# Half of the first weight loaded later, two warming products fewer, and norm factors by token turned from the finished row

## The chip, the core and the metric

The kernel runs on one core of one Trainium2 chip. The core has five engines, each with its own list of instructions that it works through in order: TensorE (PE, with PEld for the loading of its stationary operand), VectorE (DVE), ScalarE (ACT), GpSimd (POOL) and SyncE (SP, which here only issues transfers). They wait for each other on semaphores. The metric is the time of one execution on the device in microseconds (us). The kernel before took 2257.14 us, the median of three runs (2255.66 to 2258.51).

## What is computed

A decoder trunk of two layers over 1024 tokens of width 1024, with a memory of 256 tokens, all in float32. In short:

```
for l in (0, 1):
    if l == 1: shared K/V of the sparse attention = rmsnorm(x, g_kv) @ w_kv
    mem_k, mem_v = split(rmsnorm(mem, g_mem[l]) @ w_mem_kv[l])
    h = rmsnorm(x, g_mix[l])
    if l == 0:   # gated linear attention and memory attention
        q, k, v, r, alr, mq = split(h @ a_w_in)
        x = x + concat(gla(q, k, v, alr) * silu(r), mem_attend(mq)) @ a_w_out
    else:        # native sparse attention and memory attention
        x = x + concat(nsa(h, shared), mem_attend(mq)) @ b_w_out
    x = x + conv_ffn(rmsnorm(x, g_ffn[l]))
return rmsnorm(x, g_final)
rmsnorm(x, g) = x * rsqrt(mean(x * x, axis=-1) + 1e-6) * g
```

## The kernel before, in words

**Layout.** Activations lie with 128 channels on the partitions and tokens along the row: `x` is eight tiles (k = 0 to 7) of 128 channels by 1024 tokens, worked on in two halves of 512 tokens. Every operand of a dense product is split into a rounded high part and the rest (`rl`, `rl_into`, `wsplit`: ScalarE casts the high part, VectorE subtracts it), and each product is three matmuls: high by high, high by low, low by high. `projg` (L189) does this for one 128-column weight over the eight k: 24 matmuls of 128 by 512, lines L194 to L196.

**Norms.** The factor of a norm is not multiplied into the input of a product but into its output. `Norm` sums the squares of the eight tiles into two accumulators `nacc`. `done()` adds these, and one matmul with a matrix of 1/1024 (`on_d`, L287) leaves the mean square in the bank `ms`, 128 equal rows of 512 tokens. `inv_rms` (L243) makes the factors `rs` of it in six operations that each need the one before: Ln, Exp and Square on ScalarE (L246 to L248), then three on VectorE (L249 to L251).

Products whose output has tokens on the partitions (values) need the same factors as a column: `by_token` (L290) multiplies each 128 tokens of the accumulator with one column of `on_d`, four matmuls of one output column into a bank `mst`, and runs a second `inv_rms` on 128 by 4 (`rst`). It needs only the accumulator, not `rs`. The memory norm (`MemKV.norm`, L363) does it with two more columns in its own bank `mms`. There are six such places, lettered here by time in the profile:

- A, 27 us: `stats(0)`, first half of layer 0, L661 and L662, behind the third of four 24-matmul products `qk`, ahead of the fourth.
- B, 49 us: `stats(1)`, second half, between the value products `gv` of the first half.
- C, 72 us: memory norm of layer 0, between the products `mk`.
- D, 1046 us: `norm(0)` in `after_ffn0`, L1488, between the last products `dn` of the first feed-forward.
- E, 1067 us: `norm(1)`, behind the products `kc` of the first half, ahead of those of the second.
- F, 1093 us: memory norm of layer 1, behind the products `mk`, ahead of `mv`.

**The start.** PE first runs fourteen products of `on_d` with itself (`warm`, L146). `stats(0)` issues the loads on SP: x tile 0, the first half of the first weight `wqk`, x tile 1, the second half of that weight, x tiles 2 to 7. Then ScalarE and VectorE split both weight halves, and after them each x tile into `h` (L650 to L652). The first weight half holds k = 0 to 3, the second k = 4 to 7. The gain `cg` comes by ScalarE's queue.

**What sets the order.** A scheduler takes the program in the order in which it is written, with generators (`yield`) woven into each other by `blend`, and lays the instructions of each engine in a list; it may move one ahead of another whose inputs are not ready. PSUM banks come from one pool of eight (`PS`, L81), all with the tag `ps`, in the order in which the program takes them. At run time each engine follows its list.

## Time and profile before

| | |
|---|---|
| median of three runs | 2257.14 us (2255.66 to 2258.51) |
| profiled execution, first to last instruction | 2257.4 us |
| PE busy | 2215.0 us, 98% of the span |
| DVE, ACT, POOL busy | 1729.8, 1126.3, 433.6 us |
| mean granted clock of PE | 0.997 of full |
| PE's recorded waits for another engine or a transfer | about 30 us in all, the longest 2.67 us |

In a row of the timeline the first number is the start in us from the span's start, the second the busy time of the group; then engine, line, operation, output <- inputs, shape, count, and in brackets the idle time of that engine just before it with what ended it. Matmuls overlap: one of 128 by 512 shows 0.39 us, and the next starts 0.227 us after it; the distance of starts is what it costs. A float32 matmul that was not split stands as two.

### The profile page before, as it was taken

How to read it: one execution, taken by the hardware profiler on the slowest of the kernel's cores; microseconds unless marked ns; L12 is line 12 of the kernel's file. 1: busy time of each engine (PE TensorE's matmuls, PEld its weight loads, DVE VectorE, ACT ScalarE, POOL GpSimd, SP SyncE). 2: the span in 40 equal slices, each digit the busy share in tenths (PEclk: the TensorE clock that was granted, in tenths of full speed). 3: DMA queues.
4: the chain of work that ended last, by engine and by line, in shares of the span. 5: the costliest groups of instructions: out<-in, count | busy, mean ns of one | idle time of the engine just before them, and what ended most of it. 6: DMA issues, size and time to landing. Idle time of an engine off the chain costs nothing.

```text
span 2257.4 us, 31218 instructions
## 1 busy us (share of the span) xinstructions
PE 2215.0 (98%) x10994; PEld 1826.2 (81%) x10994; DVE 1729.8 (77%) x3069; ACT 1126.3 (50%) x2085; POOL 433.6 (19%) x409
## 2 busy tenths in 40 slices
PE   9999999999999999999999999999999999999997
PEld 7888887777888888888888878778777788888886
DVE  6786886888877768887756778866988877768877
ACT  5464464543333335456544788864543333334445
POOL 1222300013333210000103334420013333210000
PEclk9999999999999999999999999999999999999999
DMA  6332246333332329544421111036433333329533
GB/s 227 103 104 87 73 161 208 138 126 133 129 122 98 108 84 345 173 135 136 131 83 50 40 46 37 8 115 206 140 130 131 126 122 103 108 76 339 167 96 112
DMA packets 139451, 285.15 MB, mean 126 GB/s; under 512 B 16221, under 2 KB 22958, under 8 KB 139294
## 3 DMA queue, kind: packets, MB, share of 16 engines
q1 hardware_dynamic: 130942, 263.11, 35.5%
q0 software_dynamic: 3600, 11.65, 1.5%
q10 hardware_dynamic: 4752, 8.39, 1.0%
q8 instruction: 86, 1.41, 0.3%
q14 instruction: 71, 0.58, 0.1%
HBM read 211.27 MB, written 71.83 MB: 125 GB/s over the span
## 4 chain that ended last, share of the span: by engine, by line
PE 78%; DVE 10%; ACT 4%; DMA 4%; issue 2%; SPq 0%; POOL 0%; DVEq 0%; ACTq 0%; POOLq 0%
PE dn L1413 5%; PE dn L1414 5%; PE dn L1412 5%; PE fy L1058 5%; PE fy L1060 5%; PE fy L1059 5%; PE fx L1058 3%; PE fx L1059 3%; PE fx L1060 3%; PE fw L1060 3%; PE fw L1059 3%; PE fw L1058 3%; PE op L195 2%; PE op L196 2%; PE op L194 2%
## 5 line engine op out<-in xcount | busy, mean ns | idle before, releaser
L1413 PE MATMUL dn<-db,da 128*128 128x512 f32 (+1 forms) x628 | 242.5, 386 | 0.6 <-DVE db L1342 0.5
L1412 PE MATMUL dn<-db,da 128*128 128x512 f32 (+1 forms) x628 | 242.6, 386 | 0.2 <-ACT db L1341 0.2
L1414 PE MATMUL dn<-db,da 128*128 128x512 f32 (+1 forms) x628 | 241.7, 385 | 0.0
L1058 PE MATMUL fy<-B,Ah 128*128 128x512 f32 x496 | 194.6, 392 | 10.8 <-DVE q L1092 9.9
L1060 PE MATMUL fy<-B,Al 128*128 128x512 f32 x496 | 193.3, 390 | 0.4 <-DVE Al L1023 0.4
L1059 PE MATMUL fy<-B,Ah 128*128 128x512 f32 x496 | 193.1, 389 | 0.0
L1042 POOL TENSOR_TENSOR wu<-wu,wu 128x512 f32<-128x512 f32 x36 | 47.2, 1311 | 735.1 <-DVE Al L1023 600.5
L1022 ACT ACTIVATE Ah<-wu 128x1024 fp32r<-128x1024 f32 x124 | 130.4, 1052 | 102.8 <-PE fy L1059 60.3
L1023 DVE TENSOR_TENSOR Al<-wu,Ah 128x1024 fp32r<-128x1024 f32 x124 | 160.8, 1297 | 8.4 <-ACT Ah L1022 7.3
L1413 PEld LDWEIGHTS dn<-db,da 128*128 128x128 f32 x628 | 117.9, 188 | 26.8 <-DVE db L1342 2.8
L1412 PEld LDWEIGHTS dn<-db,da 128*128 128x128 f32 x628 | 118.0, 188 | 24.4 <-ACT db L1341 0.6
L1060 PE MATMUL fw<-B,Al 128*128 128x512 f32 x352 | 137.7, 391 | 0.0
L1058 PE MATMUL fw<-B,Ah 128*128 128x512 f32 x352 | 137.1, 390 | 0.0
L1059 PE MATMUL fw<-B,Ah 128*128 128x512 f32 x352 | 137.1, 389 | 0.0
L1414 PEld LDWEIGHTS dn<-db,da 128*128 128x128 f32 x628 | 117.9, 188 | 23.2
L1342 DVE TENSOR_TENSOR db<-bl,db 128x512 fp32r<-128x512 f32 x154 | 106.0, 688 | 28.4 <-ACT db L1341 27.9
L1058 PEld LDWEIGHTS fy<-B,Ah 128*128 128x128 f32 x496 | 93.1, 188 | 35.2 <-DVE q L1092 14.1
L1341 ACT ACTIVATE db<-bl 128x512 fp32r<-128x512 f32 x154 | 95.7, 621 | 31.3 <-PE dn L1414 20.6
L1060 PEld LDWEIGHTS fy<-B,Al 128*128 128x128 f32 x496 | 93.1, 188 | 20.6 <-DVE Al L1023 0.9
L1059 PEld LDWEIGHTS fy<-B,Ah 128*128 128x128 f32 x496 | 93.1, 188 | 18.9
L1138 ACT ACTIVATE fc<-fc 128x512 f32<-128x512 f32 x88 | 54.9, 626 | 106.3 <-DVE fc L1119 85.2
L1341 ACT ACTIVATE da<-wb 128x512 fp32r<-128x512 f32 x88 | 54.9, 628 | 101.4 <-PE dn L1413 63.9
(416 smaller groups left out, 6185.8 us busy)
## 6 DMA issues: line engine op xcount, KB each, us to landing
wu<-in_w_up_dram SPq DMA_DIRECT2D x176, 256.0 KB, 3.0
bl<-gb_d SPq DMA_DIRECT2D x154, 256.0 KB, 2.9
gb_d<-fc SPq DMA_DIRECT2D x132, 256.0 KB, 2.4
wb<-in_w_down_dram SPq DMA_DIRECT2D x44, 256.0 KB, 4.2
wa<-in_w_down_dram SPq DMA_DIRECT2D x22, 512.0 KB, 7.8
wo<-in_a_wo_dram SPq DMA_DIRECT2D x16, 512.0 KB, 3.7
xre<-om_d SPq DMA_DIRECT2D x32, 256.0 KB, 4.3
x_r<-x SPq DMA_DIRECT2D x32, 256.0 KB, 2.4
```

What stands on the lines that cost most here:

```text
L1022: a = nc.scalar.activation(hi, src, AF.Copy)
L1023: b = nc.vector.tensor_tensor(lo, src, f(hi), ALU.subtract)
L1042: tt(b1, b0, b1, ALU.add)
L1058: mm(ps, wr, hr, start=(first and j == 0), stop=False, skip_group_check=True)
L1059: mm(ps, wr, hl, start=False, stop=False, skip_group_check=True)
L1060: mm(ps, wl, hr, start=False, stop=(stop and j == 3), skip_group_check=True)
L1138: silu[0] = nc.scalar.activation(self.c[half], self.c[half], AF.Silu)
L1341: nc.scalar.activation(w[:, hs(0)], t, AF.Copy)
L1342: b = tt(w[:, hs(1)], t, f(w)[:, hs(0)], ALU.subtract)
L1412: mm(o, hi, bh, start=first, stop=False, skip_group_check=True)
L1413: mm(o, hi, bl, start=False, stop=False, skip_group_check=True)
L1414: mm(o, lo, bh, start=False, stop=stop or n == NP - 1, skip_group_check=True)
```

## The change

Three things. The load of the first weight's second half moves behind x tile 3, and its split stands just before the split of that tile, tied behind tile 2's on ScalarE. The warming products are twelve and no longer fourteen. And `by_token` becomes a function that takes the finished `rs`: TensorE turns each 128 by 128 piece of it (`transpose` with the identity, one matmul each), and VectorE copies one column of each piece out of the bank. The one-column matmuls and the second `inv_rms` are gone in all six places; the memory norm takes a bank `mst` of its own for it.

```diff
@@ -144,7 +144,7 @@
         )
 
     warm = PS("warm")
-    for _ in range(14):
+    for _ in range(12):
         mm(warm[:, :P], on_d, on_d, start=True, stop=True)
 
     def back_to_exp(after):
@@ -251,6 +251,14 @@
         nc.vector.tensor_tensor(y[:, :n], y[:, :n], a[:, :n], ALU.mult)
         return y
 
+    def by_token(rs, n):
+        pt = PS("mst")
+        for c in range(n):
+            nc.tensor.transpose(pt[:, c * P : (c + 1) * P], rs[:, c * P : (c + 1) * P], ident)
+        y = S([P, 4], s="rst", bufs=3)
+        nc.vector.tensor_copy(y[:, :n], pt[:, : n * P].rearrange("p (c q) -> p c q", c=n)[:, :, 0])
+        return y
+
     class Norm:
         def __init__(self, width=HT):
             self.acc = [None, None]
@@ -287,19 +295,6 @@
                 mm(ms, on_d, self.acc[j], start=(j == 0), stop=(j == n - 1))
             return inv_rms(ms, self.w)
 
-        def by_token(self):
-            n = self.w // P
-            pt = PS("mst")
-            for c in range(n):
-                for j, a in enumerate(self.acc):
-                    mm(
-                        pt[:, c : c + 1],
-                        a[:, c * P : (c + 1) * P],
-                        on_d[:, 0:1],
-                        start=(j == 0),
-                        stop=(j == len(self.acc) - 1),
-                    )
-            return inv_rms(pt[:, :n], n, S([P, 4], s="rst", bufs=3), S([P, 4], s="rtt", bufs=2))
 
     def gained(get, rs, gc, h, odd=(1, 3, 5, 7)):
         for k in range(KT):
@@ -365,9 +360,8 @@
             acc = self.acc
             ms = PS("mms")
             mm(ms[:, :M], on_d, acc[:, :M], start=True, stop=True)
-            for m in range(2):
-                mm(ms[:, M + m : M + m + 1], acc[:, m * P : (m + 1) * P], on_d[:, 0:1], start=True, stop=True)
-            self.rs = inv_rms(ms[:, : M + 2], M + 2)
+            self.rs = inv_rms(ms[:, :M], M)
+            self.rst = by_token(self.rs, 2)
 
         def project(self):
             M = 256
@@ -406,7 +400,7 @@
                         mm(pv[m], hl, r, start=False, stop=(k == KT - 1))
                     yield 1.3
             for m in range(2):
-                self.V.append(rl(pv[m], scale=self.rs[:, M + m : M + m + 1], s="mV"))
+                self.V.append(rl(pv[m], scale=self.rst[:, m : m + 1], s="mV"))
 
     om_d = dp.tile([KT, P, T], F32, name="om_d")
     x_r = dp.tile([KT, P, T], F32, name="x_r")
@@ -636,8 +630,8 @@
                 if half == 0:
                     for i in range(2):
                         nc.sync.dma_start(tv[:, i, :], x[2 * k2 + i, :, hs(half)])
-                        if k2 == 0:
-                            nc.sync.dma_start(raw[:, hs(i)], a_w[2, :, hs(i)])
+                        if (k2, i) in ((0, 0), (1, 1)):
+                            nc.sync.dma_start(raw[:, hs(k2)], a_w[2, :, hs(k2)])
                 else:
                     nc.gpsimd.dma_start(tv, x[2 * k2 : 2 * k2 + 2, :, hs(half)].rearrange("k p t -> p k t"))
                 tvs.append(tv)
@@ -647,8 +641,10 @@
                         k = 2 * k2 + i
                         t = V(F32R, "h")
                         h.append((t[:, :HT], t[:, HT:]))
-                        if k2 == 0:
-                            rl_into(wr[:, hs(i)], wl[:, hs(i)], raw[:, hs(i)])
+                        if (k2, i) in ((0, 0), (1, 1)):
+                            first = rl_into(wr[:, hs(k2)], wl[:, hs(k2)], raw[:, hs(k2)])
+                            if n.past is not None:
+                                follow(first, n.past, "order")
                         n.past = rl_into(*h[-1], tv[:, i, :], cg[:, k : k + 1])
                         yield 1.0
             for k2, tv in enumerate(tvs):
@@ -659,7 +655,7 @@
                     yield 0.5
             yield 2.0
             rs[half] = n.done()
-            rst[half] = n.by_token()
+            rst[half] = by_token(rs[half], 4)
             yield 1.0
 
         def second_x(h):
@@ -1487,7 +1483,7 @@
 
         def norm(half):
             rs[half] = nn[half].done()
-            rst[half] = nn[half].by_token()
+            rst[half] = by_token(rs[half], 4)
             yield 0.5
 
         hh = [[None] * KT, [None] * KT]
```

How it moves instructions. First ScalarE at the start of the program; `wqkr` is the high part of the first weight, `h` that of an x tile. Before:

```order
L230 ACTIVATE wqkr_111<-wqk_110 128x512 x2
L233 ACTIVATE h_127<-x_6_113,cg_108 128x512
L233 ACTIVATE h_132<-x_6_113,cg_108 128x512
L233 ACTIVATE h_137<-x_7_118,cg_108 128x512
L233 ACTIVATE h_140<-x_7_118,cg_108 128x512
```

And now:

```order
L230 ACTIVATE wqkr_109<-wqk_108 128x512
L233 ACTIVATE h_125<-x_6_111,cg_106 128x512
L233 ACTIVATE h_130<-x_6_111,cg_106 128x512
L233 ACTIVATE h_133<-x_7_115,cg_106 128x512
L230 ACTIVATE wqkr_109<-wqk_108 128x512
L233 ACTIVATE h_136<-x_7_115,cg_106 128x512
```

Three tiles now stand ahead of the second weight half. VectorE's list moves in the same way.

PE at place A, where `ms` is the mean square and `mst` the bank of the factors by token. Before:

```order
L196 MATMUL qk_241<-h_152,wqkl_238 128x512
L287 MATMUL ms_272<-nacc_209,on_d 128x512
L295 MATMUL mst_283<-on_d,nacc_209 128x1 x4
L194 MATMUL qk_313<-h_127,wqkr_309 128x512
L195 MATMUL qk_313<-h_127,wqkr_309 128x512
```

And now:

```order
L196 MATMUL qk_239<-h_150,wqkl_236 128x512
L295 MATMUL ms_270<-nacc_207,on_d 128x512
L257 MATMUL mst_281<-idu,rs_273 128x128 x4
L194 MATMUL qk_305<-h_125,wqkr_301 128x512
L195 MATMUL qk_305<-h_125,wqkr_301 128x512
```

The place in the list is the same, the input is not: the accumulator `nacc` before, the finished factors `rs` now. The list at E reads like this one, with `kc` for `qk`.

PE at place F, now (before, the two one-column matmuls stood right behind `mms`, and `mv` behind them):

```order
L362 MATMUL mms_8643<-macc_8486,on_d 128x256
L1587 MATMUL hid_8540<-ck_8250,wc_1090_8688 128x128
L1587 MATMUL hid_8541<-ck_8250,wc_1090_8688 128x128
L1587 MATMUL hid_8540<-ck_8250,wc_1090_8688 128x128
L1587 MATMUL hid_8541<-ck_8250,wc_1090_8688 128x128
L1587 MATMUL hid_8540<-ck_8250,wc_1090_8688 128x128
L1587 MATMUL hid_8541<-ck_8250,wc_1090_8688 128x128
L1587 MATMUL hid_8540<-ck_8250,wc_1090_8688 128x128
L1587 MATMUL hid_8541<-ck_8250,wc_1090_8688 128x128
L257 MATMUL mst_8653<-idu,rs_8645 128x128 x2
L398 MATMUL mv_8668<-wmvr_8672,mh_8392 128x512
L399 MATMUL mv_8668<-wmvl_8673,mh_8392 128x512
```

Eight `hid` products, which write banks taken earlier in the program, stand between the mean square and the turn; the `mv` products, whose bank is taken later, stand behind it. In the same way 20 `gv` matmuls stand ahead of the turn at B, 24 `mk` at C and 21 `dn` at D.

## The prediction

> **What bounds the kernel now.** I read the page first, then the waits of PE, then the timeline around each place that the change touches.
>
> ```profile
> span 2257.4 us, 31218 instructions
> PE 2215.0 (98%) x10994; PEld 1826.2 (81%) x10994; DVE 1729.8 (77%) x3069; ACT 1126.3 (50%) x2085; POOL 433.6 (19%) x409
> PE 78%; DVE 10%; ACT 4%; DMA 4%; issue 2%; SPq 0%; POOL 0%; DVEq 0%; ACTq 0%; POOLq 0%
> ...
> PE qk L194 <- ACT h L233: 1.4, 1, 1.4
> PE gr L196 <- DVE wrl L177: 1.4, 1, 1.4
> ```
>
> PE is busy for 98% of the span and is 78% of the chain that ended last. So a microsecond put into PE's list, or a microsecond for which PE stands still, is a microsecond of the kernel unless PE waits later for the same thing anyway; a microsecond saved on DVE or ACT is nothing. The sum is made against the profiled execution's 2257.4 us, which is 0.3 us over the median of the runs and inside their spread.
>
> **The start.** PE's first product waits for ACT (1.4 us above), and ACT for the second half of the first weight:
>
> ```profile
> 4.51 0.63 ACT L230 ACTIVATE wqkr<-wqk 128x512 fp32r<-128x512 f32 x1 [2.51 <-DMA wqk<-in_a_w_dram]
> 7.25 0.63 ACT L230 ACTIVATE wqkr<-wqk 128x512 fp32r<-128x512 f32 x1 [2.11 <-DMA wqk<-in_a_w_dram]
> 7.91 0.69 DVE L231 TENSOR_TENSOR wqkl<-wqk,wqkr 128x512 fp32r<-128x512 f32 x1 [2.05 <-ACT wqkr L230]
> 8.53 5.39 DVE L234 SCALAR_TENSOR_TENSOR h<-x,cg,h 128x512 fp32r<-128x512 f32 x8
> 8.55 0.50 PE L194 MATMUL qk<-h,wqkr 128*128 128x512 f32 x1 [1.35 <-ACT h L233]
> 9.34 0.50 PE L195 MATMUL qk<-h,wqkr 128*128 128x512 f32 x1 [0.29 <-DVE h L234]
> 9.68 0.40 PE L196 MATMUL qk<-h,wqkl 128*128 128x512 f32 x1
> 14.31 1.23 DVE L177 TENSOR_TENSOR wqkl<-wqk,wqkr 128x1024 fp32r<-128x1024 f32 x1 [0.33 <-ACT wqkr L176]
> 16.75 0.39 PE L196 MATMUL qk<-h,wqkl 128*128 128x512 f32 x1
> ```
>
> With the second half behind three tiles, the first `h` can follow the first half's cast, at about 5.1 us, and PE starts as soon as its twelve warming products end, near 6.3 us. That is 2.2 us earlier, but not 2.2 us gained: PE's 25th to 27th product belong to the second weight, whose low part DVE makes from 14.31 to 15.54 us. Its load stands behind the same bytes as before, so this stays. The first product that reads it started at 16.75 us; at best it starts at 15.55. Gain: at most 1.2 us, and I take 1.2, since DVE's last `h` (13.92 us before) also comes about a microsecond earlier. Nothing, if the second half's landing now holds up the tiles behind it. The two warming products fewer are not a gain of their own, because PE waits for `h` and not for them.
>
> **The turn, where nothing waits.** A turn of 512 tokens is four PE matmuls; the trace has such a group in place, at its cost per start:
>
> ```profile
> 28.03 0.95 PE L295 MATMUL mst<-on_d,nacc 128*128 128x1 f32 x8
> 28.84 0.48 PE L194 MATMUL qk<-h,wqkr 128*128 128x512 f32 x1
> ...
> 131.92 0.60 PE L838 MATMUL kdT<-idu,kd 128*128 128x128 f32 x4
> 132.28 0.48 PE L194 MATMUL mq<-h,wmqr 128*128 128x512 f32 x1
> ```
>
> The removed group cost 28.84 - 28.03 = 0.81 us, the turns cost 0.36: 0.45 us less at each of the four wide places, 0.18 less at the two memory norms (half as many). The removed operations on ACT and DVE (0.15 to 0.26 us each, six at each wide place) are off the path.
>
> **The wait that the turn adds.** The old matmuls needed the accumulator, as `ms` did, so they could follow it at once. The turn needs `rs`, behind six dependent operations, and PE's list is in order: row 9.68 above needed a weight part ready at 8.60 and an `h` used at 8.55, yet stood behind row 9.34, which waited for DVE. At A and E the turn follows `ms` directly; at F eight `hid` products are between. I read the reason from the lists: in all six places only products into banks taken before `mst` were moved ahead of the turn, and at A and E none was left.
>
> Place A, with the chain that makes `rs`:
>
> ```profile
> 28.34 0.67 ACT L246 ACTIVATE rt<-ms,epsc 128x512 f32<-128x512 f32 x1
> 30.50 0.69 DVE L249 SCALAR_TENSOR_TENSOR rt<-ms,rt 128x512 f32<-128x512 f32 x1 [2.13 <-ACT rt L248]
> 31.69 0.69 DVE L251 TENSOR_TENSOR rs<-rs,rt 128x512 f32<-128x512 f32 x1
> ```
>
> `rs` was done at 32.38; without the small operations woven between, about 0.15 us earlier, 32.2. The turn then takes 0.36 us and some 0.25 for the weight load and the start. The next `qk` goes at 32.85 where it went at 28.84: **+4.0 us** (3.8 to 4.3).
>
> Place E. Here ACT comes late to the mean square:
>
> ```profile
> 1068.00 0.95 PE L295 MATMUL mst<-on_d,nacc 128*128 128x1 f32 x8
> 1068.81 0.48 PE L194 MATMUL kc<-h,wkcr 128*128 128x512 f32 x1
> 1070.52 0.67 ACT L246 ACTIVATE rt<-ms,epsc 128x512 f32<-128x512 f32 x1
> 1074.21 0.69 DVE L251 TENSOR_TENSOR rs<-rs,rt 128x512 f32<-128x512 f32 x1
> ```
>
> PE has `ms` out by 1068.0, but ACT is in the memory's splits and squares until 1070.52 and `rs` ends at 1074.90. The change's ACT list has one more square ahead of Ln, some 0.5 us, and three small operations fewer, some 0.45; I take 1074.7. The next `kc` goes at 1075.2 instead of 1068.81: **+6.4 us** (5.5 to 7.0).
>
> Place F, with `hid` as the cover and a transfer in the chain:
>
> ```profile
> 1093.54 0.50 PE L369 MATMUL mms<-on_d,macc 128*128 128x1 f32 x4
> 1093.90 0.48 PE L404 MATMUL mv<-wmvr,mh 128*128 128x512 f32 x1
> 1096.74 1.95 PE L1591 MATMUL hid<-ck,wc 128*128 128x128 f32 x16
> 1098.44 0.48 PE L404 MATMUL mv<-wmvr,mh 128*128 128x512 f32 x1
> 1098.56 1.22 DVE L169 TENSOR_TENSOR wmq<-wmq,cs 128x1024 f32<-128x1024 f32 x1 [1.33 <-DMA wmq<-in_b_w_dram]
> 1099.70 0.29 DVE L250 TENSOR_SCALAR rt<-rt 128x258 f32<-128x258 f32 x1
> 1101.04 0.42 DVE L251 TENSOR_TENSOR rs<-rs,rt 128x258 f32<-128x258 f32 x1
> ```
>
> In the change's DVE list the scaling of `wmq` stands between the chain's second and third DVE operation, so `rs` follows it: 1099.70 + 0.4 = 1100.1, and `mv` at 1100.55. Before, `mv` went at 1093.90; the `hid` products, now ahead of it, are 1.70 us (1096.74 to 1098.44) that it no longer has behind it. 1100.55 - 1093.90 - 1.70 = 4.95. The longer standstill at E moves PE somewhat more than the loads, so I take **+4.5 us** (2.1 if the transfer and DVE are prompt, 5 at most).
>
> Places B and D, where 20 and 21 matmuls were moved ahead:
>
> ```profile
> 49.77 0.95 PE L295 MATMUL mst<-on_d,nacc 128*128 128x1 f32 x8
> 53.72 0.68 DVE L251 TENSOR_TENSOR rs<-rs,rt 128x512 f32<-128x512 f32 x1
> ...
> 1047.16 0.95 PE L295 MATMUL mst<-on_d,nacc 128*128 128x1 f32 x8
> 1052.12 0.69 DVE L251 TENSOR_TENSOR rs<-rs,rt 128x512 f32<-128x512 f32 x1
> ```
>
> Twenty matmuls at 0.227 us (two neighbours at full clock) reach from 49.77 to 54.3, against `rs` at 54.4: a wait of 0.2 us, less the 0.45 saved. At D 21 reach 1051.9 against 1052.8, which DVE reaches 0.8 us sooner because the `dn` products it waits for come 0.8 sooner. B, D and C (24 `mk` as cover, a short wait) together: **-0.4 us** (-1.2 to +0.5).
>
> **The clock.** PE's granted clock fell in two stretches after little PE work, and stayed up through a wait of 2.67 us; in these rows, each of a window of 2 us, PE's busy time stands behind the window's length, and the granted clock is the third number from the end:
>
> ```profile
> 12.00:14.00 2.00, 2.00 (x6) 1.56 (x6) 1.98 (x4) 1.57 (x3) 0.00 (x0) 0.58 1.05 364
> 76.00:78.00 2.00, 2.00 (x11) 2.00 (x11) 1.83 (x4) 0.00 (x0) 0.00 (x0) 0.50 0.51 203
> ...
> 1688.00:1690.00 2.00, 0.00 (x0) 0.00 (x0) 2.00 (x5) 1.18 (x3) 0.00 (x0) 1.00 0.88 327
> 1690.00:1692.00 2.00, 1.51 (x7) 1.25 (x8) 2.00 (x6) 1.03 (x2) 0.00 (x0) 1.00 0.53 198
> ```
>
> The first fall came after PE's 1.35 and 0.29 us of waiting, the second (75.1 to 78.5 by the distances of starts) after a stretch of tiny matmuls at C. Each lasted about 3.4 us, in which PE did half its work: 1.7 us each. The standstills at A, E and F are 4.2, 6.9 and some 4.9 us, all longer than what made the clock fall at 10 us, so I count one fall for each: **+5.1 us** (2.5 if they fall luckily, 7.5 if some last two stretches). [...]
>
> **Sum.** -1.2 + 4.0 + 6.4 + 4.5 - 0.4 = 13.3 us; with the clock's 5.1, 18.4 us. 2257.4 + 18.4 = **2275.8 us**, 0.8% slower.
>
> **Rivals.**
>
> *The waits are given back.* After A, PE waits for DVE again within the same stage (1.4 us at `gr`, in the first fence), and the long standstills let DVE and ACT run ahead; F's cover may also be better. If `gr` and the like pay back 1.4 us and F costs 2.1 (2.4 less) with one clock fall fewer (1.7), the time is 2275.8 - 5.5 = 2270.3. For it: DVE has 23% free. Against: PE shows no wait between E and 1272 us to give back.
>
> *The clock holds.* As through the 2.67 us above: 2257.4 + 13.3 = 2270.7. Against: the standstills here are longer than that one.
>
> *Not slower: PE does not stand at the turns.* If PE passed a waiting turn and went on with the products behind it, A, E and F would cost nothing, and all that is left is the start and the cheaper turns, 4 x 0.45 + 2 x 0.18 = 2.2: 2257.4 - 1.2 - 2.2 = 2254.0, within what a measurement here can tell from no change (0.2%, 4.5 us). It decides as soon as a `qk` row at A starts before `rs` ends. Against it stand rows 9.34 and 9.68. [...]
>
> *The start does not gain.* ACT, in order, now meets the second half's landing between tiles 2 and 3; if it lands late, tile 3 and all behind it wait too, and the 1.2 us are lost: 2277.0. The loads of both tiles behind it are the same bytes as before, which speaks against more than that.
>
> **How the numbers follow.** The forecast has 0.60, given back 0.15, the held clock 0.13, no standstill 0.04, the start without gain 0.08. The range is 2266 to 2282: all costs at their low ends (-1.2 + 3.8 + 5.5 + 2.1 - 1.2 + 2.5 = 11.5) give 2268.9, with some of A given back less; all at their high ends (0 + 4.3 + 7.0 + 5.0 + 0.5 + 7.5 = 24.3) give 2281.7. Slower by over 0.2% holds in every case but that of no standstill and what is not thought of: 0.95; within 0.2% 0.04; faster 0.01.
>
> **What would show it.** At A the row of the turn starts some 4 us after `ms` ends, with PE idle before it and DVE's `rs` as what ended that; the same at E with some 7 us and at F with 4 to 5, where DVE's `wmq` stands inside the chain. Granted clock near 0.5 for about 3 us behind each. At B and D a wait under 0.5 us. PE's first `qk` near 6.3 us, the second weight's first low product near 15.6. It is wrong if `ms` and the turn at E lie closer than 5 us (ACT came to Ln earlier), if F's turn finds `rs` ready, or if PE's waits later in the stage shrink by what A added.

## The result, and the profile after

The changed kernel takes 2284.33 us, the median of four runs (2282.02 to 2288.38); the kernel before took 2257.34 us beside it. The ratio is 1.0119, with a 95% interval of 1.0105 to 1.0132: slower by 27 us, where 18.4 were predicted. The time lies 8.5 us over the predicted one and 2.3 us over the top of the range.

The page of the changed kernel, with the recorded waits of PE (total, times, longest), in the order span, busy times, shares of the chain that ended last, waits:

```profile
span 2282.6 us, 31149 instructions
PE 2220.8 (97%) x10970; PEld 1827.0 (80%) x10970; DVE 1730.0 (76%) x3063; ACT 1125.8 (49%) x2073; POOL 434.5 (19%) x409
PE 76%; DVE 11%; ACT 6%; DMA 4%; issue 3%; SPq 0%; DVEq 0%; POOL 0%; ACTq 0%
...
PE mst L257 <- DVE rs L251: 16.3, 4, 7.4
PE fy L1054 <- DVE q L1088: 12.1, 7, 2.7
```

A wait that did not exist before leads the list: PE stands 16.3 us in all before the turns. The second line is the feed-forward's, which the change does not touch; it was 9.9 us before.

Places A, E and F in the timeline of the changed kernel:

```profile
25.79 1.02 PE L295 MATMUL ms<-nacc,on_d 128*128 128x512 f32 x2
30.16 0.69 DVE L251 TENSOR_TENSOR rs<-rs,rt 128x512 f32<-128x512 f32 x1
30.91 1.11 PE L257 MATMUL mst<-idu,rs 128*128 128x128 f32 x4 [4.10 <-DVE rs L251]
31.67 0.78 PE L194 MATMUL qk<-h,wqkr 128*128 128x512 f32 x1
...
1075.95 1.02 PE L295 MATMUL ms<-nacc,on_d 128*128 128x512 f32 x2
1079.99 0.67 ACT L246 ACTIVATE rt<-ms,epsc 128x512 f32<-128x512 f32 x1
1084.33 1.12 PE L257 MATMUL mst<-idu,rs 128*128 128x128 f32 x4 [7.36 <-DVE rs L251]
1085.10 0.78 PE L194 MATMUL kc<-h,wkcr 128*128 128x512 f32 x1
...
1111.15 1.95 PE L1587 MATMUL hid<-ck,wc 128*128 128x128 f32 x16
1115.96 1.22 DVE L169 TENSOR_TENSOR wmq<-wmq,cs 128x1024 f32<-128x1024 f32 x1 [2.06 <-DMA wmq<-in_b_w_dram]
1117.67 0.66 PE L257 MATMUL mst<-idu,rs 128*128 128x128 f32 x2 [4.57 <-DVE rs L251]
1117.98 0.78 PE L398 MATMUL mv<-wmvr,mh 128*128 128x512 f32 x1
```

Each turn has PE idle ahead of it, and what ended the idle time is DVE's `rs`. At E ACT comes to Ln 4 us after `ms` began, since splits and squares of the memory stand before it; at F the scaling of `wmq`, held up by its transfer, is inside the chain. The turn itself, four starts, takes 0.76 us at A (30.91 to 31.67), not the 0.36 of the place that the prediction quoted, because PE's clock is already at half. The stretches of the timeline show that (length, PE busy; the granted clock is third from the end):

```profile
30.00:32.00 2.00, 1.09 (x5) 1.09 (x6) 1.93 (x4) 0.00 (x0) 0.00 (x0) 0.50 1.02 381
32.00:34.00 2.00, 2.00 (x7) 1.52 (x6) 0.84 (x3) 0.00 (x0) 0.00 (x0) 0.50 1.02 387
34.00:36.00 2.00, 2.00 (x6) 1.60 (x5) 0.76 (x2) 1.34 (x3) 0.00 (x0) 0.50 0.87 331
36.00:38.00 2.00, 2.00 (x9) 1.56 (x8) 1.81 (x4) 2.00 (x6) 0.00 (x0) 0.84 0.02 5
512.00:514.00 2.00, 2.00 (x7) 1.52 (x6) 1.02 (x3) 0.51 (x1) 0.00 (x0) 0.50 0.25 84
532.00:534.00 2.00, 2.00 (x6) 1.55 (x5) 2.00 (x5) 0.38 (x1) 0.00 (x0) 0.50 0.65 154
```

The clock is at half up to about 36.6 us behind A, and also at 512 and 532 us, in layer 0's feed-forward, where nothing was expected.

Laying PE's rows of both kernels side by side, in order, gives how much later (+) each piece of work starts. Where that distance grows is where the time went. Such distances are medians over a few neighbouring rows, good to about 0.1 us:

| stretch (time before) | predicted | change | same kernel, second execution | turns alone |
|---|---|---|---|---|
| start, to 20 us | -1.2 | -1.4 | -1.7 | -2.1 |
| A with the clock behind it, to 35 us | +5.7 | +6.5 | +6.6 | +6.3 |
| rest of layer 0's mixing (B, C), to 450 us | part of -0.4 | -1.4 | -1.9 | +2.0 |
| feed-forward of layer 0, 450 to 640 us | 0 | **+5.5** | **+2.9** | **+2.7** |
| to E (D inside) | part of -0.4 | -0.5 | +0.3 | +1.3 |
| E with its clock | +8.1 | +8.8 | +10.0 | +9.2 |
| F with its clock, less its `hid` rows | +6.2 | +6.6 | +7.2 | +6.9 |
| layer 1 behind F | 0 | +1.0 | +2.6 | +1.8 |
| sum | 18.4 | 25.1 | 26.0 | 28.1 |

The places that the change touches, taken together, cost 18.6 us in the first execution (the sum less 5.5 and 1.0) and 20.5 in the second, near the predicted 18.4. That closeness is in part luck. A, E and F alone cost 21.9 us in the first and not 20.0, and most of what offsets this, in the rows of the start and of B and C, is that before's one trace holds two clock falls (stretches at half clock) of 1.7 us each, at 10.3 and 75.1 us, that do not come in the change's traces. What is missing besides is in work that the change does not touch.

One pair of rows from layer 0's feed-forward shows it, a wait of PE for `q` and the wait of ACT behind which it stands. Before:

```profile
519.77 0.63 ACT L1022 ACTIVATE A<-wu 128x512 fp32r<-128x512 f32 x1 [1.65 <-DMA wu<-in_w_up_dram]
522.85 0.50 PE L1058 MATMUL fy<-B,Ah 128*128 128x512 f32 x1 [1.35 <-DVE q L1092]
```

After:

```profile
527.86 0.63 ACT L1018 ACTIVATE A<-wu 128x512 fp32r<-128x512 f32 x1 [3.46 <-DMA wu<-in_w_up_dram]
530.48 0.50 PE L1054 MATMUL fy<-B,Ah 128*128 128x512 f32 x1 [2.70 <-DVE q L1088]
```

The up weights `wu` land later against the work that needs them, PE waits 1.35 us longer, and the longer wait is followed by half clock, another 1.7 us. The order of the instructions on ACT, DVE, POOL, SP and PE in this stretch is the same in both kernels.

### The profile page after: what moved, and what is told of

Read it like the earlier page. It is cut to its first block, busy times and chain, and to the rows that moved or that the text cites. A ratio compares the mean times of both kernels' runs of the same rounds, so it can differ in the third digit from the quotient of the medians.

```text
span 2282.6 us, 31149 instructions
## 1 busy us (share of the span) xinstructions
PE 2220.8 (97%) x10970; PEld 1827.0 (80%) x10970; DVE 1730.0 (76%) x3063; ACT 1125.8 (49%) x2073; POOL 434.5 (19%) x409
## 3 DMA queue, kind: packets, MB, share of 16 engines
q8 instruction: 86, 1.41, 0.3%
## 4 chain that ended last, share of the span: by engine, by line
PE 76%; DVE 11%; ACT 6%; DMA 4%; issue 3%; SPq 0%; DVEq 0%; POOL 0%; ACTq 0%
PE dn L1409 6%; PE dn L1410 6%; PE dn L1408 6%; PE fy L1054 5%; PE fy L1056 5%; PE fy L1055 5%; PE fx L1054 3%; PE fx L1055 3%; PE fx L1056 3%; PE fw L1056 3%; PE fw L1055 3%; PE fw L1054 3%; PE op L195 2%; PE op L196 2%; PE op L194 2%
```

## The experiments

The kernels were timed in four groups, each group on one chip with before beside it; the four chips differ. The last column is the ratio less one, times before's median in the same group (2257.5, 2256.8, 2255.0 and 2252.9 us). The ratio is not that of the two medians and can lie up to 1.5 us beside it: "start alone, 12 warming products" is 3.0 us over before by the medians, 4.5 by the ratio. The intervals reach 2 to 5 us to either side.

| kernel | ratio to before (95%) | us over before |
|---|---|---|
| change, second time | 1.0133 (1.0118 to 1.0149) | 30.0 |
| start alone, 12 warming products | 1.0020 (1.0006 to 1.0034) | 4.5 |
| turns alone | 1.0138 (1.0115 to 1.0161) | 31.2 |
| all turns at first use | 1.0030 (1.0016 to 1.0043) | 6.8 |
| only A at once | 1.0062 (1.0045 to 1.0079) | 14.0 |
| only E at once | 1.0076 (1.0055 to 1.0097) | 17.2 |
| only F at once | 1.0055 (1.0034 to 1.0075) | 12.4 |
| change, 34/62/34 spare products | 1.0149 (1.0129 to 1.0169) | 33.6 |
| change, 18/32/20 spare products | 1.0093 (1.0072 to 1.0114) | 21.0 |
| bank taken early, 1 spare product | 1.0057 (1.0040 to 1.0074) | 12.9 |
| bank taken early, 7/4/1 spare products | 1.0027 (1.0014 to 1.0041) | 6.1 |
| before, 7 warming products | 1.0036 (1.0020 to 1.0052) | 8.1 |
| turns at first use, 19 warming products | 1.0014 (1.0000 to 1.0028) | 3.2 |
| start alone, 14 warming products | 1.0009 (0.9999 to 1.0020) | 2.0 |
| before, 21 warming products | 1.0005 (0.9995 to 1.0015) | 1.1 |

One run of the kernel with all turns at first use took 7856.6 us and is left out of its ratio.

### The parts apart

**The start alone**: the change without its `by_token`.

> The change's start alone (twelve warming products, the second half of the first weight behind three tiles), with the factors by token summed as before. Theory (the loss is PE standing behind the turns, and the clock that falls behind it): no standstill, so the start's gain is all that is seen: the first qk near 6.1 us, the second weight's first low product near 15.3, and the time 1.2 to 1.5 us under before's 2257.3, that is 2255.8 to 2256.1. Rival (the start loads the early stages otherwise, and the later surplus in layer 0's feed-forward comes from the moved start): the two fy rows that waited 2.6 and 2.7 us in the change's feed-forward wait so here too, and the time is 2260 or more.

Its trace agrees with the theory (no standstill, the second `fy` row waits 0.2 us, work 0.7 us earlier at 27 us), but its time does not: 2260.5 us, 4.5 over before, where 1.2 to 1.5 less was expected. The rival's time came, without the rows that it gave as the reason. One trace shows one execution, and this one was the fastest of ten (2255.74 to 2267.25). Nor are the 0.7 us a gain of the start: before's trace, beside which they are read, was itself late there (see the start in the section on the prediction).

**The turns alone**: the change with before's start.

> The turns alone, with before's start (fourteen warming products, the second half behind the first tile). Theory: the whole loss stays and the start's gain is gone: 2284.3 + 1.4 = 2285.7 us, with standstills of some 4, 7 and 4.5 us before the turns at A, E and F. Rival (the start takes part in the loss): at least 5 us under the change, 2279 or less. If the surplus of 5.3 us in layer 0's feed-forward hangs on how far PE is moved against the loads, it differs from the change's own, since PE is here 1.4 us later.

2288.6 us against 2286.7 of the change in the same group: the loss is the turns'. In the trace PE stands 4.10, 7.37 and 4.76 us at A, E and F.

**Every turn at its first use.** The edit, shortened; it is the same in `values` of layer 1 and in `MemKV.project`:

```diff
 # stats(half), norm(half):
-            rst[half] = by_token(rs[half], 4)
 # values(half), among its products:
+                    if k == 5 and rst[half] is None:
+                        rst[half] = by_token(rs[half], 4)
```

> The whole change, but every turn is made where its factors are first read (among the value products of each half, and among the mv products of a memory layer), so that rs has long been done when PE comes to the turn. Theory (PE's standing behind the turn is the loss, not the turn's own work): A, E and F lose their standstills and clock falls; what is left is the start's gain and the cheaper turns: 2254 us (2252 to 2256), and no mst row waits 0.5 us. Rival (the turn itself, its copy on DVE and the longer life of rs cost the time): the loss stays in part, 2265 or more. Rival (the surplus in layer 0's feed-forward comes from elsewhere): 2259 or more, with fy waits of 2.6 us.

No `mst` row waits any more, as the theory said. PE's rows of the tile `mst` (count, duration in ns, first and last start; then what they waited for, which is nothing, and what waited for them):

```profile
L258 PE MATMUL mst<-idu,rs x20: 270/272/273, 53.6 to 1314.7; 128*128 128x128 f32 x20
its engine sat idle before it (us, times) until:
who waited for it (us, times):
  DVE rst L260: 0.2, 1
```

But 2265.2 us is 6.8 over before, and 2254 was expected. The standstills are 23 of the change's 30 us; the other 7 are a loss that the prediction did not have. 2265 or more is also what the first rival named, the turns' own cost and their other place in the lists, so this run does not rule it out. The trace is again of one of the quicker executions (span 2258.7) and shows little of the loss: ACT waits 2.80 us for the up weights, but PE behind it hardly longer than before (1.44 us against 1.35).

**The change once more**, unaltered.

> The change itself once more, for a second execution in the trace. Theory A (layer 0's feed-forward loses 5.3 us because of where this one execution's clock windows and transfers fell): the two fy waits or the clock falls behind them differ here, and the surplus between 450 and 640 us against before is under 3 us. Theory B (the surplus follows from the kernel's order and its shift of PE): the same two fy rows wait 2.6 us again, both clock falls come again, and the surplus is 4.5 to 6 us. The time is 2284 in either case, give or take 2.

Between the two theories: the second `fy` row waits 2.69 us again with half clock behind it, the first 1.85 and not 2.63 us without. The surplus is 2.9 us, so one half of the 5.5 repeats, and the other was of the one execution.

### One place at a time, and the clock

Each of the three kernels is the one with all turns at first use, but with one turn again directly behind its mean square.

> The kernel with every turn at its first use, but the turn of place A (the first half's factors, in layer 0's first stage) again directly behind ms. Theory (each standstill is a loss of its own, and they add): the kernel with all turns late took 2265.2 us; A adds what PE lost there in the change's traces, 4.2 us of standing and 2.3 us of half clock, so 2271.7 us, and 2274.5 if the 2.8 us in layer 0's feed-forward come with A's shift of PE (then the second fy row waits 2.7 us and ACT 3.4 us for the up weights there, as in all three traces with A's turn at once). Rival (the surplus in the feed-forward is an accident of an execution): the fy row waits 1.4 us or less, and the time is near 2271.7. Rival (the loss is given back later in the layer): under 2269.

> The kernel with every turn at its first use, but the turn of place E (the first half's factors, behind layer 0's feed-forward) again directly behind ms. Theory: 7.4 us of standing and 1.3 to 2 us of half clock, about 9 us on the 2265.2 us of the kernel with all turns late: 2274.4 us. Layer 0's feed-forward lies ahead of it and has no A before it: the second fy row there waits 1.4 us or less. Rival (E's standstill lets the loads and DVE run ahead, and layer 1 gives part of it back): under 2270.

> The kernel with every turn at its first use, but the turn of place F (the factors of layer 1's memory) again directly behind mms and the eight hid products. In the change's traces PE lost 6.5 us there, 4.6 to 4.8 of it standing. Theory: without E's standstill ahead of it rs is no earlier against PE, so about the same here: 2265.2 + 6.5 = 2271.7 us. Rival (F was long only because E had moved PE against the loads): half of it, 2268.5 or less, with a wait of 2.5 us or less at the mst row.

Measured 2270.95, 2274.61 and 2268.26 us: over the kernel with no standstill A costs 14.0 - 6.8 = 7.2 us, E 10.4, F 5.6. With the 6.8 they add to 30.0, which is what the change itself measured in the first group. So good an agreement is luck, by the intervals; but it fits separate losses of which none is given back, and in the table no later stretch shrinks by what A, E or F added. F's median lies at its rival's, but the rival's wait of 2.5 us is not what the row shows. (The trace is of the slowest of five runs, 2276.42 us; three others took 2267.6 to 2268.3.)

```profile
1105.26 0.69 PE L258 MATMUL mst<-idu,rs 128*128 128x128 f32 x2 [5.83 <-DVE rs L252]
```

In the feed-forward the theory's tie to A fell: A at once had ACT wait 1.66 us for the up weights, and only F at once, with no standstill ahead of the feed-forward, 3.34 us.

**Spare products in the standstill.** In `by_token`, ahead of the transposes:

```diff
+        for _ in range(fill):
+            mm(pt[:, :P], on_d, on_d, start=True, stop=True)
```

> The change with spare products of on_d with itself ahead of the turns at A (34), E (62) and F (34), into the bank that the turn then overwrites, so that PE works while rs is made; nothing else is changed. Theory (a standstill costs its length and besides the half clock behind it): the turns start when they did, to within 0.5 us, the clock holds behind A, E and F, and the time is the change's 2286.7 less 5.2, near 2281.5 us. Rival (the clock falls for reasons that PE's idle time does not set): falls of 3.4 us stay behind A, E and F, and the time stays within 1.5 us of the change's. Rival (the spare products delay the turn): more than 2288.

I had taken half of what such a product costs; 34 of them (68 rows) hold PE 7.75 us:

```profile
26.81 7.75 PE L257 MATMUL mst<-on_d 128*128 128x128 f32 x68
34.41 0.60 PE L259 MATMUL mst<-idu,rs 128*128 128x128 f32 x4
```

So the turns came late and the time rose, the last rival's case. The clock held, but this run does not price it. It was made again with fewer (18, 32, 20):

> The change with spare products ahead of the turns again, but fewer (18 at A, 32 at E, 20 at F): the kernel with 34, 62 and 34 showed that one of them takes 0.228 us, twice what was reckoned, so that they themselves set the length, and its clock held. Theory (half clock behind the standstill costs 2.3 us at A, 1.3 to 2 at E, 1.6 at F): the turns start when the change's do, the clock holds behind them, and the time is 5 us under the change's 2286.7, near 2281.5; if the instruction packet is also moved off the up weights' transfer (22 matmuls more than before ahead of the feed-forward), 2278.5. Rival (the clock costs nothing beside the standing): 2285 or more.

```profile
27.82 4.18 PE L257 MATMUL mst<-on_d 128*128 128x128 f32 x36
32.09 0.66 PE L259 MATMUL mst<-idu,rs 128*128 128x128 f32 x4
```

```profile
30.00:32.00 2.00, 2.00 (x18) 1.81 (x17) 1.78 (x3) 1.16 (x3) 0.00 (x0) 1.00 0.98 367
32.00:34.00 2.00, 1.92 (x12) 1.66 (x12) 1.94 (x5) 0.00 (x0) 0.00 (x0) 1.00 0.99 391
34.00:36.00 2.00, 2.00 (x10) 1.66 (x9) 0.14 (x1) 0.21 (x1) 0.00 (x0) 1.00 1.04 395
```

Here PE does useless work for as long as it stood (`ms` to the turn is 5.12 us at A, as in the change), and the clock stays at full behind A, E and F: 2274.9 us, 21.0 over before and so 9.0 under the change, where 8 were expected with the packet out of the way. Side by side with the change's second trace A is 2.7 us shorter, E 3 us, F 0.6 (PE still waited 2.07 us there); the feed-forward of layer 0 has lost 3.4 us, since the `fy` wait and the fall behind it are gone. Beside the first trace they are 2.7, 1.7 and 0.1 us. The clock's price is thus 4 to 6 us at the three places together, around the predicted 5.1.

### What delays the up weights

The DMA view of the stretch from the transfer's issue to the end of ACT's wait shows it. A queue's row gives packets, MB and the share of 16 engines, a transfer's row the count, KB each and the median us from issue to landing. Before (516.4 to 519.8 us):

```profile
q1 hardware_dynamic: 359, 0.67, 63.6%
wu<-in_w_up_dram SPq DMA_DIRECT2D x2, 256.0 KB, 3.5
```

After (522.7 to 527.9 us):

```profile
q1 hardware_dynamic: 322, 0.60, 44.5%
q8 instruction: 1, 0.02, 3.0%
wu<-in_w_up_dram SPq DMA_DIRECT2D x2, 256.0 KB, 5.3
```

A packet of another queue is among the up weights' packets, and they land 5.3 us after issue, not 3.5. By its count that queue carries PE's instructions: before, it has 86 packets of 16 KB (1.41 MB) in a span with 21,988 matmuls and weight loads, 255.7 to a packet, and 88 in the kernel with 34, 62 and 34 spare products, which has 22,460, 255.2 to a packet:

```profile
q8 instruction: 88, 1.44, 0.3%
```

So in these traces a packet comes once per about 256 of PE's matmuls and weight loads, that is per 128 matmuls, wherever the list then stands: before, 211 to 298 of them begin between one packet and the next, 254 in the middle; after, 192 to 311, and 254. The change's list has 14 matmuls fewer ahead of the feed-forward (four in the warm-up, four each at A and B, two at C; a float32 matmul counts as two, as in the 68 rows of the 34 spare products). 14 times 0.227 us is 3.2 us, an estimate of how much later a packet comes against the work. Measured, the packet that began at 513.6 us before, 2.8 us ahead of the transfer's issue, now begins 1.1 us behind it, 3.9 us later.

Two kernels differ in spare products alone, and so in the list's length. In both the bank `mst` is taken early, by one-column products of `on_d` that the turn overwrites, one at each of A, E and F, or seven, four and one:

```diff
+        for _ in range(fill):
+            mm(pt[:, :1], on_d, on_d[:, :1], start=True, stop=True)
```

> The change with one spare one-column product of on_d written into the turn's bank at A, E and F before the turn (it is overwritten). PE's order then has the four transposes of A 18 qk products later, those of E 21 kc products later and those of F 18 products later; all else stands where the change has it. Theory (a turn holds PE because the products behind it are placed behind the first use of its bank, and this first use waits for rs): no mst row waits 0.5 us, no clock fall behind A, E and F, and the change's 2286.7 us lose 6.5 + 9.2 + 6.7 = 22.4: 2264 us, beside the 2265.2 of the kernel with the turns at their first use. Rival (the standstill is the chain to rs, and the products now ahead of the turn only wait in their turn): 2275 or more. New theory for layer 0's feed-forward (PE's instructions come in packets of 16 KB, one for every 256 instructions of its list; the change's list is shorter, so one packet falls into the transfer of the up weights that ACT waits for, which then lands 5 us after issue and not 3.4): this kernel has 12 matmuls fewer than before ahead of the feed-forward, the packet of some 2 us is inside that transfer, ACT waits over 2.5 us.

> As the kernel with one spare product, but with seven of them at A and four at E (each is two matmuls in PE's list): with these PE's list has as many matmuls ahead of layer 0's feed-forward as before's, and as many ahead of layer 1's. New theory (the packets of PE's instructions meet the transfers in a bad place because the list is shorter): the packet near the second fy row is back ahead of the transfer, at about 512 to 515 us by before's clock, ACT waits 1.7 us for the up weights and PE 1.4 us or less, there is no clock fall there, and the time is 4 us or more under the kernel with one spare product, 2256 to 2260. Rival (the feed-forward's surplus is an accident of each execution, or comes from the turns' other order on ACT and DVE): the same time as with one spare product to within 2 us, though the kernel has 18 matmuls more.

With one product the packet is in the transfer (landing 4.5 us, ACT's wait 2.68 us); with seven it is not:

```profile
q1 hardware_dynamic: 306, 0.57, 54.3%
wu<-in_w_up_dram SPq DMA_DIRECT2D x2, 256.0 KB, 3.2
```

ACT waits 1.26 us there, PE under 0.8 us, the clock holds, and the kernel with 18 matmuls more is 5.4 us faster in the same group (2261.3 against 2266.6). The theory asked for 4 or more, but the two traces show only 1.3 us of it at this place; with one product PE waited 1.35 us there, as before did, and no fall followed. As to the turns, the first expectation held at A, where 18 products now pass ahead of the turn and it waits for nothing, but not at E and F, where the 21 and 18 products ahead end 2.20 and 1.56 us before `rs` does:

```profile
1075.95 0.66 PE L259 MATMUL mst<-idu,rs 128*128 128x128 f32 x4 [2.20 <-DVE rs L251]
```

This shows that it was the bank's first use that held the products back: one tiny product into it ahead of the turn, and the scheduler puts others in front. The change's loss falls by more than half, to 12.9 us.

The counterpart has no turn at all, only before with fewer warming products:

```diff
-    for _ in range(14):
+    for _ in range(7):
```

> The kernel before with 7 warming products in place of 14, and nothing else: its list of PE is 14 matmuls shorter ahead of everything, as the change's is ahead of layer 0's feed-forward. PE waits for its first h in either case, so the start moves by 2 us at most (a clock window more or less). New theory (the place of PE's instruction packets against the transfers): in layer 0's feed-forward the transfer of the up weights meets the packet, ACT waits 2.7 to 3.4 us for it where before waited 1.65, and the time is 3 to 5 us over before's, 2260 to 2262. Rival (accident, or the turns' own order): ACT waits 1.7 us as before, and the time is before's plus what the start loses, 2257 to 2259.

```profile
521.66 0.63 ACT L1022 ACTIVATE A<-wu 128x512 fp32r<-128x512 f32 x1 [3.37 <-DMA wu<-in_w_up_dram]
524.35 0.50 PE L1058 MATMUL fy<-B,Ah 128*128 128x512 f32 x1 [2.69 <-DVE q L1092]
```

```profile
q1 hardware_dynamic: 355, 0.66, 41.5%
q8 instruction: 1, 0.02, 3.0%
wu<-in_w_up_dram SPq DMA_DIRECT2D x2, 256.0 KB, 5.2
```

Seven warming products fewer at 1 us bring, at 524 us, the very rows of the change: the packet in the transfer, ACT's 3.37 us, PE's 2.69, half clock behind, 2.9 us in all. The time rose by 8.1 us, more than the 3 to 5 expected, and the list's length is not all that differs. PE stood 3.07 us for its first `h`, and its products then start 0.43 us apart, which is half clock, up to 13.3 us, where the other traces reach full clock by 7.1 us. The `ms` at A starts at 26.8 us, 1.6 to 1.7 later than in the traces of the same start with 14 and 21 products and no fall (25.1 and 25.2). The traced execution ends 1.1 us behind before's, so what the others lost beyond this is not seen.

### The length put back

> The kernel with every turn at its first use, with 19 warming products in place of 12: 14 matmuls more, so that PE's list is as long as before's ahead of layer 0's feed-forward. They end about 1.5 us later, of which the wait of 1.1 us or more that PE has near 10 us takes most. Theory (the list's length places the packets of PE's instructions): the packet near 514 us is ahead of the up weights' transfer, ACT waits under 2 us for it, and the time is 3 to 6 us under the 8 us by which the kernel with 12 warming products was slower than before: 2 to 5 us over before. Rival (the turns' other order on ACT and DVE costs the 8 us): 7 us over before or more.

> The change's start alone, but with before's 14 warming products: the second half of the first weight behind three tiles, PE's list as long as before's. Theory (the start gains 0.7 to 1.5 us at the second weight's first low product, and the shorter list took it back elsewhere): 1 us under before to level with it, between 0.9993 and 1.0002 of it. Rival (the moved load itself costs something later): 3 us or more over before, as with 12 warming products.

> The kernel before with 21 warming products in place of 14, and nothing else: they end near 8.7 us, as PE's first h comes (8.5 us), so the start costs 0.3 us at most. PE's list is 14 matmuls longer, and a packet of its instructions comes about 3 us earlier against the work. Theory (only a packet on a transfer that is waited for costs): near 515 us it is further ahead of the up weights' transfer, ACT waits 1.7 us or less, and the time is before's to within 2 us, unless a packet falls on another such transfer; then a wait for the up weights of 2.7 us or more shows at that place. Rival (the kernel before was fitted to its length as a whole, any other costs 5 us): 2260 or more.

Measured 3.2, 2.0 and 1.1 us over before. In all three traces ACT waits 1.26 to 1.50 us for the up weights, and the packet is ahead of them. The first went from 6.8 to 3.2 us as expected, and its rival of 7 or more fell; the second from 4.5 to 2.0, over what was expected, and its interval (0.9999 to 1.0020) holds "level" and leaves no room for a gain of more than 0.2 us; the third is level, so not any other length costs. Taken one by one, the intervals of the pairs with 12 and with 14 or 19 warming products overlap; the pair with one and seven spare products, and before with 7 and with 21, do not or hardly do. No kernel here is shown to beat the one before.

## Why the prediction was wrong, point by point

- **A**: right in mechanism; 4.2 us of standing against 4.0, 2.3 of half clock against 1.7. The 0.25 us for the turn's weight load and start was the author's estimate; the trace has `rs` end at 30.85 us and the turn's first row at 30.91, 0.06 us later. Put alone into the kernel without standstills it costs 7.2 us.
- **E**: right in mechanism, under-sized by about 1 us: the next `kc` came 9.15 us behind the start of `ms` and not 8.1, since the turn, reckoned at 0.36 us, ran at half clock and took 0.77, and ACT was later still at Ln.
- **F**: 4.8 us of standing against 4.5, and the `wmq` scaling inside the chain as said.
- **B, C, D**: the waits were under 0.3 us as said; the stretches around them gained more than the 0.4, by luck: before's own clock fall at C, 1.7 us, did not come again in the change's traces, and came in others.
- **The clock**: 5.1 us predicted, 5.2 in the first trace as net loss behind A (2.3), E (1.3) and F (1.6). The rival in which it holds fell. One fall was counted for each standstill longer than the 1.35 and 0.29 us of waiting ahead of the fall at 10 us, and in the change's first trace one came at each, of 6.8 us and not 3.4, part of it while PE stood. Only E's follows a window of 3.413 us (the grid of the last section) that was idle throughout: the window ahead of A's fall had PE busy for 0.12 of it and the one ahead of F's for 0.37. In the feed-forward the clock fell behind waits of 2.63 and 2.70 us, with PE busy for 0.45 and 0.32 of the window ahead. The length of a wait alone does not decide (last section).
- **The start**: the term was read from an execution that was late there by itself, and the 1.4 us of the table are no gain of the change: the turns alone, which keep before's start, have 2.1 in the same row. In before's trace ACT waits 2.11 us for the first weight's second half, the clock falls at 10.3 us, and DVE begins the second weight's low part at 14.31 us, which the prediction took as fixed. The turns alone, with the same start, and the change:

```profile
6.00 0.63 ACT L230 ACTIVATE wqkr<-wqk 128x512 fp32r<-128x512 f32 x1 [0.96 <-DMA wqk<-in_a_w_dram]
13.24 1.23 DVE L177 TENSOR_TENSOR wqkl<-wqk,wqkr 128x1024 fp32r<-128x1024 f32 x1 [0.44 <-ACT wqkr L176]
...
8.36 0.63 ACT L230 ACTIVATE wqkr<-wqk 128x512 fp32r<-128x512 f32 x1 [0.61 <-DMA wqk<-in_a_w_dram]
13.97 1.22 DVE L177 TENSOR_TENSOR wqkl<-wqk,wqkr 128x1024 fp32r<-128x1024 f32 x1 [0.94 <-ACT wqkr L176]
```

  In the three other traces with before's start (turns alone, before with 7 and with 21 warming products) DVE's row begins at 13.20 to 13.38 us and no fall comes at 10 us; in the thirteen with the moved half it begins at 13.36 to 15.18, 14.42 in the middle. With the moved load the row thus comes later in these traces, by about 1 us in the middle, and not earlier. The times agree that nothing is gained: alone the start was 4.5 us slower than before, with before's number of warming products level with it, and beside the turns it is worth 1.9 us by the medians (2288.6 against 2286.7), within their spread. Two warming products fewer were put at nothing; whether they cost through the list's length is not shown: with 12 the start alone has ACT wait only 1.52 us for the up weights.
- **No standstill, waits given back**: both fell. The `gr` wait went from 1.4 to 1.2 us, and the three places, put back one by one, add up to 23.2 us.
- **The step that failed** is the rest of the sum, what stands in it beside A, E and F: a gain of 1.2 us at the start and of 0.4 at B, C and D, and nothing for work that the change does not touch, which was silently taken to last what it lasted. The kernel without any standstill is made of just these parts, and it was 6.8 us slower where the sum has it 1.6 us faster: 8.4 us. A, E and F were right in mechanism and under-sized, 23.2 us by the runs where 20.0 stand in the sum. Of the untouched work 2.9 us are seen in both of the change's traces: PE's shorter list puts an instruction packet on the up weights' transfer in layer 0's feed-forward, PE waits 1.35 us longer behind it, and a clock fall follows. For the rest no cause is shown; it differs between executions of one kernel. The range was built from the terms' own bounds and so could not hold it.
- **A slip without weight**: a run's time is its span and 1.75 to 1.80 us, in all profiled runs here, so the execution seen of before took 2259.2 us by the same measure, 2 over the median and above the highest of its runs (2258.51), and not 2257.4. The difference of the spans, 25.2 us, is for that reason less than the 27.0 of the medians.

What stays open: of the 7 us that the kernel without any standstill lost, putting the list's length back recovered about half by the medians, with intervals that overlap, and its trace shows PE losing next to nothing to the packet; whether the turns' other place in the lists has a part in it was not tested apart; why the moved half makes the second weight later; and what the other executions of the shorter lists lost beyond what the traces show.

## What to carry to other kernels

A product that needs a late result should not be written where the result is asked for but where its output is read, or its bank should be taken by something that need not wait; otherwise PE stands with all that is queued behind it, 4.10, 7.36 and 4.57 us here, and pays the clock besides, 5.2 us net. In a kernel whose PE is busy for 97% of the span, removing a dozen tiny matmuls can cost more than they did (bank taken early: the kernel with 18 matmuls fewer is 5.4 us slower); one way, seen here, is that the instruction packets move against transfers that are waited for (the up weights land 5.3 us after issue, not 3.5). Such a change is judged on several executions, with the waits for transfers of untouched stages laid beside those of before. A gain read from one trace, like the start's, should be seen in a second trace of the same kernel first. And a sum of terms needs a term for the work that is not touched, at least as wide as the kernel's own executions differ (2249.8 to 2259.9 us for before in one group).

## What the runs showed that was not expected

- An instruction packet cost time here. Near this place but off the transfer one takes 0.9 to 1.7 us; on the up weights' transfer 2.0 to 2.5 us, and the transfer lands 4.5 to 5.3 us after issue instead of 3.2 to 3.5. Of the nine traces of kernels with 10 to 14 matmuls fewer than before ahead of the feed-forward, the packet began 0.9 to 1.4 us after the transfer's issue in eight, and ACT waited 2.7 to 3.5 us; PE then waited 2.7 us in five of them and 1.4, as before did, in three. In the ninth (only A at once, with as short a list) it began 2.4 us after the issue, and ACT waited 1.66 us. In the eight other traces ACT waited 1.3 to 1.7 us; in seven the packet was over before the issue or not near it, in one (start alone, 12 warming products) it began 0.6 us before the issue. So it hurt only where it began within those 0.9 to 1.4 us.
- PE's clock changed on a grid. In every one of the 17 traces, all changes of the granted clock lie a whole number of 3.413 us after the first one, and a fall lasted one such window (1.7 us of PE's work) or several; A, E and F took one to three, part of them while PE stood. How long a single wait was did not tell whether a fall followed: after 2.63 and 2.70 us it came (after, 511 and 531 us) and after 0.88 us (turns alone, 457 us), after 2.67 us (before, 1690 us) and 1.85 us (the change again, 508 us) it did not. Cut by this grid (the last 12 us of each trace left out), the busy time of PE's rows tells more: in all 27 windows at full clock in which PE was busy for less than 0.42 of the window the clock was halved in the next, and of the 11,104 with 0.43 or more in 14. So in these traces a wait was followed by a fall when enough of it lay within one window, and where the grid lies differs between them (a fall begins at 10.28 us in before's trace and at 29.81 in the change's, 5.72 windows apart).
- A float32 product of 128 by 128 cost 0.228 us at full clock as one of a row of them (7.75 us for 34, in the run with 34, 62 and 34 spare products).
